# Feature tiles and seven products in a fixed order, and seven separate sums in the second layer, in a two-layer DiT trunk

## The chip, the cores and the metric

The kernel runs on one core of a Trainium2 chip. The metric is the device time of one execution in microseconds (us). Before the change three runs gave 1634.02, 1637.30 and 1638.63 us, a median of 1637.3 us.

## The reference

The reference is a trunk of two layers over 512 latent tokens and 256 context tokens of width 1024. Each layer has a mixer part (four head groups behind one input projection, one output projection) and an MLP with a squared ReLU, each with a modulated LayerNorm in front and a LayerNorm behind. The change lies in the MLP alone:

```
def channel_mlp(h, w1, w2):
    return jnp.square(jax.nn.relu(h @ w1)) @ w2      # 1024 -> 4096 -> 1024

x = layer_norm_affine(DN_ALPHA * x + m[2] * y, ln1_g[l], ln1_b[l])
f = channel_mlp(modulate(x, m[3], m[4]), w_ff1[l], w_ff2[l])
x = layer_norm_affine(DN_ALPHA * x + m[5] * f, ln2_g[l], ln2_b[l])
```

The second layer has no context tokens in its MLP, since only the latent stream is returned. So N, the number of tokens in the MLP, is 768 in the first layer and 512 in the second.

## The kernel before

All matrix products keep float32 accuracy by splitting each operand into a rounded part and a rest: `mm3` (L135) issues three matmuls (hi*hi, hi*lo, lo*hi) for each product of 128 rows. A weight tile therefore arrives by DMA as "raw", ScalarE copies it to "hi" (L162, L1307), and VectorE subtracts to get "lo" (L165, L1308).

The 4096 features of the MLP are worked in eight chunks of 512 (`ffn`, L1181). A **feature tile** (`ff1`, L1212) is 128 features for all tokens: 8 x 3 matmuls of 512 columns, and in the first layer 8 x 3 more of 256 columns for the context; ScalarE's ReLU reads it out of PSUM (L1199). Seven chunks, 0 to 6, of the second product go through a scheme with **seven products** in place of eight (Winograd's form of Strassen's): `operands` (L1256) squares the tiles on GpSimd (L1262), forms sums of halves of the tokens on GpSimd (L1281), and splits seven left operands (L1274 and L1275, tiles "fop"); `weights` (L1287) does the same with four quarters of the weight chunk (differences on GpSimd at L1312); `ff2_chunk` (L1323) multiplies. One product is HT blocks of 128 tokens (HT is 3 in the first layer, 2 in the second), each of 2 x 3 matmuls of 512 columns into one PSUM bank. Behind each bank VectorE adds it into SBUF (L1338), into one or two of the sums "acc" and "base"; the first time a sum is written ScalarE copies it (L1336). Per chunk that is 10 additions of 128x512 for each of the HT blocks, in both layers.

The last chunk is computed directly: four feature tiles, squared as hi and lo (`square`, L1201), and `ff2_tile` (L1371) with 12 matmuls for each tile of 128 tokens and 512 outputs, 12 such tiles in the first layer and 8 in the second. Before they can be added, the sums are finished: "base" is added (L1418), GpSimd multiplies by the gate row (L1419), and VectorE adds the residual "rawx", which comes back from DRAM (L1420). The residual loads, the last weights and the weights of the chunks share one pool of four raw buffers (`N_RAW`, tag "raw").

Who does what when: the kernel is written in program order and a scheduler orders the instructions of each engine ahead of time; each engine then runs its list in order. TensorE's order in this part is the scheduler's, too (`self.pin` is None). DMAs that go through `bcast_rows` (L1434) are issued from ScalarE's list and keep their place in program order; the gate rows of the second half of the layer come through it, by `rows2(0)`, right behind the first feature tiles. The lines that hold this:

```
    rs = ff1_first()
    big = [self.G([128, 1024], "base") for _ in range((HT + 1) // 2)]
    gl, gc = rows2(0)
    ...
    for c in range(NCH - 1):
        if c < NCH - 2:
            ops = operands(ff1(c + 1))
        ff2_chunk(c, left, acc, base, more)
    rs = ff1(NCH - 1)
```

Of the kernel before, what the change touches and what calls it, by code (L numbers as in the profile page):

```python
# [9 lines left out]
F32 = mybir.dt.float32  # L10
F32R = mybir.dt.float32r
AF = mybir.ActivationFunctionType
ALU = mybir.AluOpType
# [5 lines left out]
NL = 512  # L19
# [28 lines left out]
class Trunk:  # L48
# [105 lines left out]
    def load_w(self, pieces, shape, name, gate=None):  # L154

        nc = self.nc
        raw = self.pr.tile(shape, F32, name=self.nm("raw" + name), tag="raw")
# [1023 lines left out]
    def ffn(self, l, hL, hC, x, xc, rows2, mod2, done):  # L1181
# [6 lines left out]
        def ff1_w(f):  # L1188
            W = self.load_w([((slice(None),), w1[:, :, 128 * f:128 * f + 128])], [128, 8, 128], "w1",
                            self.gate if f < 8 else None)  # L1190
            return [[W[j][:, k, :] for j in range(2)] for k in range(KT)]
# [20 lines left out]
        def ff1(c):  # L1212
            rs = []
            for f in range(4 * c, 4 * c + 4):
                W = ff1_w(f)
                ps = self.P2("ff1")
                ff1_mm(ps[:, :NL], hL, 0, W)
                if full:
                    ff1_mm(ps[:, NL:NL + NC], hC, 0, W)
                r = self.T("relu", 768)  # L1220
                relu(r, 0, ps[:, :N])
                rs.append(r)
            return rs
# [32 lines left out]
        def operands(rs):  # L1256

            pool = nc.gpsimd  # L1260
            for r in rs:
                pool.tensor_tensor(out=r[:, :N], in0=r[:, :N], in1=r[:, :N], op=ALU.mult)  # L1262
            q = []
            for p in range(2):
                tmp = self.T("fsum", 768)
                e, o = rs[2 * p], rs[2 * p + 1]
                q.append((e[:, :half], o[:, :half], e[:, half:N], o[:, half:N], tmp[:, :half], tmp[:, half:N]))

            def halves(k):
                res = []  # L1270
                for v in q:
                    z = self.Z("fop")
                    hi, lo = z[:, :half], z[:, half:N]
                    nc.scalar.activation(out=hi, in_=v[k], func=AF.Copy)  # L1274
                    nc.vector.tensor_tensor(out=lo, in0=v[k], in1=hi.bitcast(F32), op=ALU.subtract)  # L1275
                    res.append((hi, lo))
                return res

            def sums(o, a, b, op):
                for v in q:  # L1280
                    pool.tensor_tensor(out=v[o], in0=v[a], in1=v[b], op=op)  # L1281

            yield halves(0)
            sums(4, 2, 3, ALU.add)
            yield halves(4)
            sums(5, 4, 0, ALU.subtract)
            yield halves(5)  # L1287
            sums(4, 1, 5, ALU.subtract)
            yield halves(4)
            sums(2, 0, 2, ALU.subtract)  # L1290
            yield halves(2)
            yield halves(1)
            yield halves(3)

        def weights(c):

            pool = nc.gpsimd
# [13 lines left out]
            def diff(o, a, b):  # L1311
                pool.tensor_tensor(out=o, in0=a, in1=b, op=ALU.subtract)  # L1312

            b11, b12, b22, b21 = raw(0, 0), raw(0, 1), raw(1, 1), raw(1, 0)
            yield halves(b11)
            diff(b11, b12, b11)
            yield halves(b11)
            diff(b11, b22, b11)
            yield halves(b11)
            diff(b12, b22, b12)  # L1320
            yield halves(b22)
            yield halves(b12)
            yield halves(b21)  # L1323
            diff(b21, b21, b11)
            yield halves(b21)

        def ff2_chunk(c, left, acc, base, more):


            B = weights(c)  # L1330
            seen = set()

            def add(ps, key, sl):
                if c == 0 and key not in seen:
                    seen.add(key)
                    nc.scalar.activation(out=sl, in_=ps, func=AF.Copy)  # L1336
                else:
                    nc.vector.tensor_tensor(out=sl, in0=ps, in1=sl, op=ALU.add)  # L1338

            for i, to in enumerate((("11", "B"), ("12", "22"), ("B",), ("12",), ("21", "22"), ("11",), ("21",))):  # L1340
                if i % 2 == 0:
                    banks = [self.PA("ff2") for _ in range(HT)]
                else:
                    big = self.P2("ff2")
                    banks = [big[:, 0:512], big[:, 512:1024]]
                    if HT > 2:
                        banks.append(self.PF("ff2") if i == 3 else self.P2("ff2")[:, 0:512])
                W, a = next(B), left[i]
                for t in range(HT):
                    for p in range(2):  # L1350
                        self.mm3(
                            banks[t], [h[:, 128 * t:128 * t + 128] for h in a[p]],
                            [h[:, p, :] for h in W], p == 0, p == 1,
                        )
                    for q in to:
                        if q == "B":
# [41 lines left out]
        for c in range(NCH - 1):  # L1398
            nxt, ops = [], None
            if c < NCH - 2:  # L1400
                ops = operands(ff1(c + 1))
                nxt += [next(ops), next(ops)]
# [262 lines left out]
```

## Time and profile before

| what | us |
|---|---|
| median of three runs | 1637.3 |
| the profiled execution | 1640.47 |
| its span, first to last instruction | 1638.4 |
| TensorE busy in the span | 1484.5 (91%) |
| VectorE busy | 1102.6 (67%) |
| ScalarE busy | 661.7 (40%) |
| GpSimd busy | 600.9 (37%) |
| chunk loop of the first layer, first tile of chunk 1 to first matmul of the last product | 436.8 to 921.3 |
| the same of the second layer | 1266.1 to 1595.5 |

The profile is one execution; it is 3.2 us longer than the median of the runs. Matmuls are pipelined in it: two in a row overlap, so the spacing of their starts, not their duration, tells what one costs. The chunk loops and the direct last chunk are more than half of the span.

### The profile page before, as it was taken

The numbers are of one execution on the slowest core, as the hardware profiler recorded it, in microseconds if no ns is written. First come the engines' busy times: TensorE is split into PE (matmuls) and PEld (weight loads), VectorE is DVE, ScalarE is ACT, GpSimd is POOL, SyncE is SP. The second block draws the span as 40 slices with busy tenths as digits, with TensorE's granted clock in tenths as the row PEclk, the third lists the DMA queues.
The fourth block names the chain that finished last, engine by engine and source line by source line (L and its number), as shares of the span: only waits on it lengthen the run. The fifth ranks groups of instructions, "written<-read, shape, count | busy, mean of one in ns | idle before, by whom it ended". The sixth has DMA issues, their size and how long they took to land. (4 is left out here: it accounts for less than half of the span.)

```text
span 1638.4 us, 23881 instructions
## 1 busy us (share of the span) xinstructions
PE 1484.5 (91%) x9228; PEld 1226.5 (75%) x9228; DVE 1102.6 (67%) x1811; ACT 661.7 (40%) x1207; POOL 600.9 (37%) x478
## 2 busy tenths in 40 slices
PE   5899889999999899999997989989989999898895
PEld 3689667787988687787876767867778778777674
DVE  3384655566574847648399589575465877678896
ACT  3433455425562323323221355355436643334331
POOL 1021333233363252432525151143242655443633
PEclk9999899999999999999999889999998999999997
DMA  8442366265212302123014423245265122233152
GB/s 287 142 117 63 122 217 193 80 223 179 78 39 65 98 29 80 39 64 91 28 62 128 130 78 116 65 149 162 86 217 179 52 89 91 81 100 103 52 154 77
DMA packets 150954, 180.45 MB, mean 110 GB/s; under 512 B 9096, under 2 KB 96568, under 8 KB 150840
## 3 DMA queue, kind: packets, MB, share of 16 engines
q1 hardware_dynamic: 140792, 160.42, 31.3%
q10 hardware_dynamic: 10048, 18.49, 3.4%
q8 instruction: 73, 1.20, 0.3%
q14 instruction: 41, 0.34, 0.1%
HBM read 169.43 MB, written 9.46 MB: 109 GB/s over the span
## 5 line engine op out<-in xcount | busy, mean ns | idle before, releaser
L133 PE MATMUL ff<-hiw,fop 128*128 128x512 f32 x980 | 325.0, 406 | 36.3 <-DVE acc L1338 35.6
L133 PEld LDWEIGHTS ff<-hiw,fop 128*128 128x128 f32 x980 | 191.3, 195 | 87.9 <-DVE acc L1338 25.3
L133 PE MATMUL ff<-hh,hiw 128*128 128x512 f32 (+1 forms) x672 | 241.6, 360 | 13.6 <-DVE acc L1338 9.5
L1308 DVE TENSOR_TENSOR low<-raww,hiw 128x1024 fp32r<-128x1024 f32 x98 | 136.7, 1397 | 159.7 <-ACT hiw L1307 159.4
L133 PE MATMUL ff<-hl,hiw 128*128 128x512 f32 (+1 forms) x672 | 240.4, 358 | 0.0
L133 PE MATMUL ff<-hh,low 128*128 128x512 f32 (+1 forms) x672 | 239.4, 356 | 0.7 <-DVE low L165 0.7
L1262 POOL TENSOR_TENSOR relu<-relu 128x768 f32<-128x768 f32 (+1 forms) x56 | 91.2, 1631 | 318.3 <-ACT relu L1199 318.3
L133 PE MATMUL ff<-low,fop 128*128 128x512 f32 x490 | 199.2, 406 | 6.7 <-DVE low L1308 6.7
L1307 ACT ACTIVATE hiw<-raww 128x1024 fp32r<-128x1024 f32 x98 | 103.2, 1060 | 231.6 <-PE ff L133 157.7
L1338 DVE TENSOR_TENSOR acc<-ff,acc 128x512 f32<-128x512 f32 x260 | 167.9, 676 | 12.3 <-PE ff L133 12.2
L1312 POOL TENSOR_TENSOR raww<-raww,raww 128x1024 f32<-128x1024 f32 x56 | 137.3, 2452 | 86.7 <-DVE low L1308 67.5
L133 PEld LDWEIGHTS ff<-hh,hiw 128*128 128x128 f32 x672 | 128.8, 192 | 36.0 <-issue 13.6
L133 PEld LDWEIGHTS ff<-hh,low 128*128 128x128 f32 x672 | 128.0, 190 | 19.2 <-DVE low L165 1.1
L133 PEld LDWEIGHTS ff<-hl,hiw 128*128 128x128 f32 x672 | 128.8, 192 | 18.0
L162 ACT ACTIVATE hiw<-raww 128x1024 fp32r<-128x1024 f32 x64 | 66.5, 1057 | 143.0 <-PE ff L133 103.2
L133 PEld LDWEIGHTS ff<-low,fop 128*128 128x128 f32 x490 | 95.5, 195 | 32.1 <-DVE low L1308 13.0
L547 POOL TENSOR_SCALAR p<-p,rec 128x768 f32<-128x768 f32 (+3 forms) x80 | 63.4, 796 | 143.1 <-DVE rec L546 133.4
L1275 DVE TENSOR_TENSOR fop<-relu,fop 128x384 fp32r<-128x384 f32 (+1 forms) x112 | 87.0, 801 | 39.9 <-ACT fop L1274 39.9
L165 DVE TENSOR_TENSOR low<-raww,hiw 128x1024 fp32r<-128x1024 f32 x64 | 82.0, 1289 | 14.6 <-ACT hiw L162 14.5
L133 PE MATMUL ada<-wada,sc 128*32 128x128 f32 x1536 | 62.4, 300 | 22.5 <-DMA wada<-in_w_ada 22.5
L1275 DVE TENSOR_TENSOR fop<-fsum,fop 128x384 fp32r<-128x384 f32 (+1 forms) x84 | 75.0, 914 | 7.3 <-ACT fop L1274 7.3
L1274 ACT ACTIVATE fop<-relu 128x384 fp32r<-128x384 f32 (+1 forms) x112 | 50.2, 466 | 68.1 <-POOL relu L1262 34.3
(362 smaller groups left out, 3237.7 us busy)
## 6 DMA issues: line engine op xcount, KB each, us to landing
raww<-in_w_ff SPq DMA_DIRECT2D x120, 512.0 KB, 4.2
wada<-in_w_ada SPq DMA_DIRECT2D x96, 512.0 KB, 4.6
rawwo<-in_w_out SPq DMA_DIRECT2D x16, 512.0 KB, 7.7
rawx<-xr SPq DMA_DIRECT2D x10, 512.0 KB, 3.4
rawz<-in_w_ff SPq DMA_DIRECT2D x8, 512.0 KB, 4.6
xr<-x SPq DMA_DIRECT2D x8, 512.0 KB, 5.1
rawwb<-in_w_in SPq DMA_DIRECT2D x12, 256.0 KB, 4.3
gate<-grow ACTq DMA_DIRECT2D x6, 512.0 KB, 7.2
```

What stands on the lines that cost most here:

```text
L133: return self.pinned(self.nc.tensor.matmul(out, lhsT, rhs, start=start, stop=stop))
L162: i = nc.scalar.activation(out=hi, in_=raw, func=AF.Copy)
L165: nc.vector.tensor_tensor(out=lo, in0=raw, in1=hi.bitcast(F32), op=ALU.subtract)
L547: nc.gpsimd.tensor_scalar(out=p[:, :keep], in0=p[:, :keep], scalar1=rec, scalar2=1.0, op0=ALU.mult, op1=ALU.mult)
L1262: pool.tensor_tensor(out=r[:, :N], in0=r[:, :N], in1=r[:, :N], op=ALU.mult)
L1274: nc.scalar.activation(out=hi, in_=v[k], func=AF.Copy)
L1275: nc.vector.tensor_tensor(out=lo, in0=v[k], in1=hi.bitcast(F32), op=ALU.subtract)
L1307: nc.scalar.activation(out=hi, in_=t, func=AF.Copy)
L1308: nc.vector.tensor_tensor(out=lo, in0=t, in1=hi.bitcast(F32), op=ALU.subtract)
L1312: pool.tensor_tensor(out=o, in0=a, in1=b, op=ALU.subtract)
L1338: nc.vector.tensor_tensor(out=sl, in0=ps, in1=sl, op=ALU.add)
```

## The change

- `ff1` becomes `ff1_tile`, one feature tile a call. The loop writes out an order for every chunk: "f01f23f45f6", where f is a feature tile of the next chunk and a digit is one of the seven products of this one. In chunk 6 the order is "01f23f456ff", and the feature tiles are those of the direct last chunk. `self.pin` is set over the loop, so TensorE runs in just this order.
- The raw weights of feature tiles in the loop come into pool "G" (4 buffers of 128x1024, shared with "base" and the gate rows) in place of the pool "raw". So that buffers of G are free, `rows2(0)`, the load of the gate rows, moves from the start of the loop to behind it.
- `operands` takes two tiles at a time, and the squares go from GpSimd to ScalarE.
- The seven products come in another order, with their sums in other places. In the second layer each product has a sum of its own, over all seven chunks (one addition a block in place of 10 for seven products); they are combined behind the loop by seven additions of 128x512 for each of two blocks. The first layer keeps its 10 additions a block.
- The last product's banks, and those of products 1, 3 and 5, come from other PSUM pools.

The core of the diff:

```diff
-        def ff1(c):
-            rs = []
-            for f in range(4 * c, 4 * c + 4):
-                W = ff1_w(f)
...
+        def ff1_tile(f, spare):
+
+            W = ff1_w(f, spare)
+            ps = self.P2("ff1")
...
-        raw = self.pr.tile(shape, F32, name=self.nm("raw" + name), tag="raw")
+        raw = self.G(shape, "raw" + name) if spare else self.pr.tile(
+            shape, F32, name=self.nm("raw" + name), tag="raw")
...
-            for r in rs:
-                pool.tensor_tensor(out=r[:, :N], in0=r[:, :N], in1=r[:, :N], op=ALU.mult)
+            for r in (e, o):
+                nc.scalar.activation(out=r[:, :N], in_=r[:, :N], func=AF.Square)
...
-            for i, to in enumerate((("11", "B"), ("12", "22"), ("B",), ("12",), ("21", "22"), ("11",), ("21",))):
+        TO = (("11", "B"), ("12",), ("11",), ("12", "22"), ("B",), ("21", "22"), ("21",)) if full else (
+            ("11",), ("12",), ("2",), ("22",), ("6",), ("7",), ("21",))
...
-        gl, gc = rows2(0)
...
+        self.pin = True
         for c in range(NCH - 1):
...
+            B = weights(c)
+            rs, nxt = [], []
+            order = "f01f23f45f6" if c < NCH - 2 else "01f23f456ff"
+            for o in order:
+                if o != "f":
+                    product(int(o), B, left, acc, base, seen)
+                    continue
+                rs.append(ff1_tile(4 * c + 4 + len(rs), True))
+                if c < NCH - 2 and len(rs) % 2 == 0:
+                    nxt.append(operands(*rs[-2:]))
             left = nxt
-
-        rs = ff1(NCH - 1)
+        self.pin = None
+
+        gl, gc = rows2(0)
+
+        def plus(o, a):
+            nc.vector.tensor_tensor(out=o, in0=o, in1=a, op=ALU.add)
+
+        for t in range(0 if full else HT):
+            c11, c12, c21, c22 = (place(acc, base, q, t) for q in ("11", "12", "21", "22"))
+            p2, p6, p7 = (base[q][t] for q in ("2", "6", "7"))
+            plus(p6, c11)
+            plus(c11, p2)
+            plus(c12, c22)
+            plus(c12, p6)
+            plus(p7, p6)
+            plus(c21, p7)
+            plus(c22, p7)
```

How this moves instructions is shown at three places. The first is TensorE's list in the first layer, inside chunk 1 (ff1 and ff2 are PSUM banks of a feature tile and of a product, hiw and low are weights, fop a left operand, hh and hl the layer's input). Before, behind two products, the last bank of one and the first of the next:

```order
L133 MATMUL ff2_1224_5788<-hiw2_1225_5790,fop_1139_5239 128x512
L133 MATMUL ff2_1237_5864<-low2_1239_5867,fop_1155_5322 128x512
L133 MATMUL ff2_1237_5864<-hiw2_1238_5866,fop_1155_5322 128x512
L133 MATMUL ff2_1237_5864<-hiw2_1238_5866,fop_1156_5325 128x512
L133 MATMUL ff2_1237_5864<-low2_1239_5867,fop_1156_5325 128x512
L133 MATMUL ff2_1229_5826<-hiw2_1232_5830,fop_1149_5283 128x512
L133 MATMUL ff2_1229_5826<-low2_1233_5831,fop_1149_5283 128x512
```

The same place in the changed kernel, behind products 0 and 1:

```order
L133 MATMUL ff2_1199_5585<-hiw2_1200_5587,fop_1137_5181 128x512
L133 MATMUL ff2_1199_5585<-hiw2_1200_5587,fop_1173_5442 128x512
L133 MATMUL ff2_1199_5585<-low2_1201_5588,fop_1173_5442 128x512
L133 MATMUL ff2_1199_5585<-hiw2_1200_5587,fop_1173_5442 128x512
L133 MATMUL ff1_1205_5618<-hh_884_4127,hiw1_1203_5614 128x512
L133 MATMUL ff1_1205_5618<-hl_885_4128,hiw1_1203_5614 128x512
L133 MATMUL ff1_1205_5618<-hh_884_4127,low1_1204_5615 128x512
```

Before, all seven products of a chunk follow one another, and four feature tiles follow these; now a feature tile stands between products 1 and 2, 3 and 4, 5 and 6, and 6 and the next 0.

The second place is ScalarE's list in the first layer where the gate rows are loaded (relu and fh are a feature tile and its squared hi part, gate and ln2g are rows broadcast from DRAM, hiw2 a split weight). Before, at the start of the loop:

```order
L1199 ACTIVATE relu_1046_4597<-ff1_1085_4868 128x256
L1199 ACTIVATE relu_1047_4599<-ff1_1085_4868 128x256
L1437 DMA gate_1088_4921<-grow_990_4403 128x1024
L1437 DMA gate_1089_4923<-grow_992_4405 128x1024
L1274 ACTIVATE fop_1101_4947<-relu_1046_4597 128x384
```

In the changed kernel, behind the loop:

```order
L1200 ACTIVATE relu_1594_8361<-ff1_1593_8312 128x768
L1204 ACTIVATE fh_1614_8471<-relu_1594_8361 128x768
L1200 ACTIVATE relu_1599_8418<-ff1_1598_8369 128x768
L1440 DMA gate_1600_8420<-grow_990_4403 128x1024
L1440 DMA gate_1601_8422<-grow_992_4405 128x1024
L1440 DMA ln2g_1608_8457<-in_ln2_g 128x1024
L1440 DMA ln2b_1609_8459<-in_ln2_b 128x1024
L1204 ACTIVATE fh_1616_8476<-relu_1599_8418 128x768
L163 ACTIVATE hiw2_1619_8483<-raww2_1618_8481 128x1024
```

The two gate loads stood behind the ReLUs of the first four tiles of the layer; now they stand behind the ReLU of its last, 32nd feature tile.

The third place is VectorE's list in the first layer at the end of the loop (fl is the lo part of a squared tile, rawx the residual, low2 the lo part of a weight of the direct last chunk). Before:

```order
L1420 TENSOR_TENSOR acc_1095_4935<-acc_1095_4935,rawx_1605_8439 128x1024
L1420 TENSOR_TENSOR acc_1096_4936<-acc_1096_4936,rawx_1606_8445 128x1024
L165 TENSOR_TENSOR low2_1620_8484<-raww2_1618_8481,hiw2_1619_8483 128x1024
L1420 TENSOR_TENSOR acc_1097_4937<-acc_1097_4937,rawx_1607_8451 128x1024
L1204 TENSOR_TENSOR relu_1586_8251<-relu_1586_8251 128x768
L1205 TENSOR_TENSOR fl_1611_8462<-relu_1586_8251,fh_1610_8461 128x768
```

In the changed kernel:

```order
L1205 TENSOR_TENSOR relu_1599_8418<-relu_1599_8418 128x768
L1206 TENSOR_TENSOR fl_1617_8477<-relu_1599_8418,fh_1616_8476 128x768
L1423 TENSOR_TENSOR acc_1088_4926<-acc_1088_4926,rawx_1602_8424 128x1024
L1423 TENSOR_TENSOR acc_1089_4927<-acc_1089_4927,rawx_1603_8429 128x1024
L1423 TENSOR_TENSOR acc_1090_4928<-acc_1090_4928,rawx_1604_8434 128x1024
L1423 TENSOR_TENSOR acc_1091_4929<-acc_1091_4929,rawx_1605_8439 128x1024
L1423 TENSOR_TENSOR acc_1092_4930<-acc_1092_4930,rawx_1606_8445 128x1024
L166 TENSOR_TENSOR low2_1620_8484<-raww2_1618_8481,hiw2_1619_8483 128x1024
L1423 TENSOR_TENSOR acc_1093_4931<-acc_1093_4931,rawx_1607_8451 128x1024
L166 TENSOR_TENSOR low2_1623_8490<-raww2_1621_8487,hiw2_1622_8489 128x1024
```

The six residual additions stood ahead of the squares of the layer's last four feature tiles; now they stand behind the square of the very last one, and the last weights' lo parts among and behind them.

## Rows read from the trace of the kernel before

**Rows 1.** The page's first part: busy us, share of span, instructions
```profile
PE 1484.5 (91%) x9228; PEld 1226.5 (75%) x9228; DVE 1102.6 (67%) x1811; ACT 661.7 (40%) x1207; POOL 600.9 (37%) x478
```
**Rows 2.** PE's waits in tile ff, 436.8 to 921.3: releaser, us, times
```profile
  DVE acc L1338: 23.9, 24
  ACT relu L1199: 4.0, 1
```
**Rows 3.** PE's waits in tile ff, 1266.1 to 1595.5: releaser, us, times
```profile
  DVE acc L1338: 21.2, 9
```
**Rows 4.** PE timeline: start, us, instruction, count, [idle before]; first matmuls of stretches
```profile
436.76 0.40 PE L133 MATMUL ff<-hh,hiw 128*128 128x512 f32 x1
...
453.44 0.40 PE L133 MATMUL ff<-hiw,fop 128*128 128x512 f32 x1
...
457.55 0.39 PE L133 MATMUL ff<-hh,hiw 128*128 128x512 f32 x1
...
602.88 0.40 PE L133 MATMUL ff<-hiw,fop 128*128 128x512 f32 x1
...
638.14 0.47 PE L133 MATMUL ff<-hh,hiw 128*128 128x512 f32 x1 [0.44 <-DVE acc L1338]
...
921.26 0.40 PE L133 MATMUL ff<-hiw,fh 128*128 128x512 f32 x1
...
1266.13 0.40 PE L133 MATMUL ff<-hh,hiw 128*128 128x512 f32 x1
...
1277.04 0.62 PE L133 MATMUL ff<-hiw,fop 128*128 128x512 f32 x2
...
1279.76 0.39 PE L133 MATMUL ff<-hh,hiw 128*128 128x512 f32 x1
...
1595.50 0.39 PE L133 MATMUL ff<-hiw,fh 128*128 128x512 f32 x1
```
**Rows 5.** Windows: stretch, length, busy us by engine, PEclk, DMA share, GB/s
```profile
630.00:633.00 3.00, 3.00 (x10) 2.38 (x9) 3.00 (x6) 0.00 (x0) 0.00 (x0) 0.62 0.69 177
```
**Rows 6.** By line: mean or ns min/median/max of one; additions, squares, gate products
```profile
L1338 DVE TENSOR_TENSOR acc<-ff,acc 128x512 f32<-128x512 f32 x260 | 167.9, 676 | 12.3 <-PE ff L133 12.2
L1262 POOL TENSOR_TENSOR relu<-relu 128x768 f32<-128x768 f32 (+1 forms) x56 | 91.2, 1631 | 318.3 <-ACT relu L1199 318.3
L1419 POOL TENSOR_TENSOR acc<-acc,gate x10: 2772/3304/3382, 870.5 to 1585.4; 128x1024 f32<-128x1024 f32 x10
L1420 DVE TENSOR_TENSOR acc<-acc,rawx x10: 1206/1217/3420, 879.0 to 1592.8; 128x1024 f32<-128x1024 f32 x10
```
**Rows 7.** PE timeline at the ends of the layers
```profile
902.07 0.80 PE L133 MATMUL ff<-hh,hiw 128*128 128x512 f32 x1 [4.00 <-ACT relu L1199]
...
958.54 0.39 PE L133 MATMUL ff<-hiw,fl 128*128 128x512 f32 x1
...
1623.02 0.39 PE L133 MATMUL ff<-hiw,fl 128*128 128x512 f32 x1
```
**Rows 8.** ACT timeline at the end of the first layer
```profile
900.26 1.06 ACT L162 ACTIVATE hiw<-raww 128x1024 fp32r<-128x1024 f32 x1 [25.72 <-DMA raww<-in_w_ff]
```
**Rows 9.** DMA: KB each, median us to landing (page); gate rows 436 to 470
```profile
raww<-in_w_ff SPq DMA_DIRECT2D x120, 512.0 KB, 4.2
gate<-grow ACTq DMA_DIRECT2D x6, 512.0 KB, 7.2
...
DMA to landing us min/median/max: 4.1/4.1/4.1
```
**Rows 10.** By line: splits of weights, squares on ACT, sums on POOL
```profile
L162 ACT ACTIVATE hiw<-raww 128x1024 fp32r<-128x1024 f32 x64 | 66.5, 1057 | 143.0 <-PE ff L133 103.2
L165 DVE TENSOR_TENSOR low<-raww,hiw 128x1024 fp32r<-128x1024 f32 x64 | 82.0, 1289 | 14.6 <-ACT hiw L162 14.5
L1203 ACT ACTIVATE fh<-relu x8: 632/732/848, 902.0 to 1598.9; 128x768 fp32r<-128x768 f32 x4, 128x512 fp32r<-128x512 f32 x4
L1281 POOL TENSOR_TENSOR fsum<-relu,relu x28: 732/1012/1713, 440.4 to 1528.0; 128x384 f32<-128x384 f32 x14, 128x256 f32<-128x256 f32 x14
```

More of the change, by code (lines that the diff above doesn't have):

```diff
@@ L1254, in ff1_first, with operands @@
             return rs
-        def operands(rs):
+        def operands(e, o):
             pool = nc.gpsimd
-            for r in rs:
-                pool.tensor_tensor(out=r[:, :N], in0=r[:, :N], in1=r[:, :N], op=ALU.mult)
[L1263 to L1293, printed above, removed]
@@ L1318, in weights @@
             diff(b11, b22, b11)
[L1319 to L1322, printed above, removed]
             yield halves(b21)
[L1324 to L1338, printed above, removed]
-            for i, to in enumerate((("11", "B"), ("12", "22"), ("B",), ("12",), ("21", "22"), ("11",), ("21",))):
[L1341 to L1356, printed above, removed]
-                            sl = base[t]
-                        else:
-                            n = int(q[1]) - 1
-                            sl = acc[HT * (int(q[0]) - 1) + t][:, 512 * n:512 * n + 512]
-                        add(banks[t], (q, t), sl)
-                more()
@@ new lines, in weights, with place, product @@
+            diff(b21, b21, b22)
+            for t in (b12, b22, b11, b21):
+                yield halves(t)
+        TO = (("11", "B"), ("12",), ("11",), ("12", "22"), ("B",), ("21", "22"), ("21",)) if full else (
+            ("11",), ("12",), ("2",), ("22",), ("6",), ("7",), ("21",))
+        def place(acc, base, q, t):
+            if len(q) == 1:
+                return base[q][t]
+            n = int(q[1]) - 1
+            return acc[HT * (int(q[0]) - 1) + t][:, 512 * n:512 * n + 512]
+        def product(i, B, left, acc, base, seen):
+            if i in (0, 2, 4, 6):
+                banks = [self.PA("ff2") for _ in range(HT)]
+            else:
+                big = self.P2("ff2")
+                banks = [big[:, 0:512], big[:, 512:1024]]
+                if HT > 2:
+                    banks.append(self.PF("ff2"))
+            W = next(B)
+            for t in range(HT):
+                ps = banks[t]
+                for p in range(2):
+                    self.mm3(
+                        ps, [h[:, 128 * t:128 * t + 128] for h in left[p][i]],
+                        [h[:, p, :] for h in W], p == 0, p == 1,
+                    )
+                for q in TO[i]:
+                    sl = place(acc, base, q, t)
+                    if (q, t) in seen:
+                        nc.vector.tensor_tensor(out=sl, in0=ps, in1=sl, op=ALU.add)
+                    else:
+                        seen.add((q, t))
+                        nc.scalar.activation(out=sl, in_=ps, func=AF.Copy)
@@ L1388, in ffn @@
         rs = ff1_first()
-        big = [self.G([128, 1024], "base") for _ in range((HT + 1) // 2)]
-        base = [big[t // 2][:, 512 * (t % 2):512 * (t % 2) + 512] for t in range(HT)]
-        gl, gc = rows2(0)
         xr = self.pd.tile([N, D], F32, name=self.nm("xr"), tag=self.nm("xr"))
@@ L1415, in ffn @@
             for n in range(2):
-                if j >= HT or n:
+                if full and (j >= HT or n):
                     sl = t[:, 512 * n:512 * n + 512]
-                    nc.vector.tensor_tensor(out=sl, in0=sl, in1=base[j % HT], op=ALU.add)
+                    nc.vector.tensor_tensor(out=sl, in0=sl, in1=base["B"][j % HT], op=ALU.add)
             nc.gpsimd.tensor_tensor(out=t, in0=t, in1=gl if j < LT else gc, op=ALU.mult)
```

64 lines of the change are left out of this document (39 added, 25 removed).

## The prediction, made before the run

> **What bounds the kernel now.** The page's first part comes first: TensorE is busy for 91% of the span, no other engine over 67% [rows 1]. So the time is TensorE's work, its waits and its clock, and the next view is what TensorE waits for in the chunk loops: VectorE's additions at L1338, 23.9 us in the first layer and 21.2 in the second, plus 4.0 once for a ReLU [rows 2, 3]. A bank can be written again only when its addition has read it, and seven products in a row fill banks faster than VectorE empties them.
>
> Waits are not the whole loss. Starts of matmuls give the price of undisturbed work [rows 4]: in the first layer two feature tiles take 453.44 - 436.76 = 16.68 us, so one costs 8.34, and the product behind them 457.55 - 453.44 = 4.11. In the second layer one feature tile costs (1277.04 - 1266.13) / 2 = 5.455 and a product 2.72. Later the seven products of one chunk take 638.14 - 602.88 = 35.26 us in place of 7 x 4.11 = 28.8. [...]
>
> A whole loop at undisturbed prices (28 feature tiles and 49 products) would be 28 x 8.34 + 49 x 4.11 = 434.9 us in the first layer; it takes 921.26 - 436.76 = 484.5, so 49.6 are lost. In the second it would be 28 x 5.455 + 49 x 2.72 = 286.0; it takes 329.4, and 43.4 are lost. **93.0 us** is therefore all that a better order of the loops can give.
>
> **The change: the order in the loops.** With a feature tile behind every two products, a bank's next use comes at least one feature tile later (8.34 or 5.46 us). One bank's additions are one or two of 0.676 us [rows 6]. In the first layer VectorE has 30 additions in a chunk as before, 20.3 us, but now over 62 us of TensorE work (4 x 8.34 + 7 x 4.11) rather than in a burst of 28.8. Two products of 3 blocks leave at most 12 additions, 8.1 us, beside the 8.34 that cover them. In the second layer a chunk has 14 additions in place of 20: 9.5 us, not 13.5. I count these waits as gone, and with them the low clock behind them.
>
> What stays is an estimate. At a loop's start the first product stands behind one feature tile and no longer behind two. It needs ReLU, a square of 0.73 and splits; the second needs four sums on GpSimd of 0.73 to 1.71 each [rows 10]. At the worst that is 0.73 + 4 x 1.71 = 7.6 us and two splits, against 8.3 and a product: some 4.5 us late in the first layer, 4 in the second. Between chunks 5 and 6 no feature tile stands in front of product 0, about 1 us in each layer; and 0.3 for each of the other 12 chunks or so. Together 14 us, from 4 (the start-up alone, half hidden) to 35 (2.5 for every chunk). The loops **gain 93 - 14 = 79**, bounds 58 and 89.
>
> **Squares.** 56 of 1.631 us leave GpSimd [rows 6]; on ScalarE one should cost 0.63 to 0.85, as L1203's squares do [rows 10]. ScalarE is 40% busy [rows 1], and 56 x 0.73 = 41 us lie beside TensorE's work: nothing. **Combination.** Behind the second loop VectorE does 14 additions where it did 6, 8 x 0.676 = 5.4 us more. They need the last products only, and two feature tiles (10.9 us) follow these: nothing, at the most 5. **Weights in G** need the same loads of 4.2 us [rows 9], with a tile's time for each to hide in: nothing.
>
> **The change: the gate rows, a new wait.** The two gate loads now stand in ScalarE's list behind the ReLU of the last feature tile. The residual's work stands behind them: a gate product on GpSimd, an addition of rawx on VectorE. The rawx loads hold all four raw buffers, and the last weights need the same buffers. So the first direct tile must wait for several gate products. Before, the loads had landed a whole loop earlier. What a late load does in this place the trace shows on a smaller scale: ScalarE's copy hiw waited 25.72 us for a raw load with ReLU behind it, and TensorE then idled 4.00 us [rows 7, 8].
>
> Call T the end of the last feature tile in the first layer. ReLU 0.8, issue 0.4 and landing 4.1 put the gate at T + 5.3; I take 5.5. (4.1 is what these loads took in an undisturbed stretch; the median of the kind is 7.2 [rows 9].) GpSimd's products follow at 2.77 to 3.38, say 3.15, the addition is 1.21 [rows 6]. The third buffer comes free at T + 5.5 + 3 x 3.15 + 1.2 = T + 16.2; a load of 4.2, hi 1.06 and lo 1.29 [rows 9, 10] put the first usable weight at T + 22.8. The two others follow 3.15 apart in their gate products; the fourth load needs the first one's buffer, so its lo is ready about T + 30.3. Two direct tiles wait for it, the second ends at T + 31.5, and ten more at 2.72 (12 matmuls, as many as a product of the second layer) give T + 58.7. Before, the twelve took 958.54 - 921.26 = 37.3 from first to last start [rows 4, 7]. That is 21 more, and a restart at the low clock adds about 1: **+22** (17 to 30).
>
> In the second layer there are four gate products: gate at T + 5.3, lo parts at 17.2, 20.3, 22.5 and 25.6, the second direct tile ends at 26.8, and six at 2.72 give T + 43. Before: 1623.02 - 1595.50 = 27.5 [rows 4, 7]. **+16** (12 to 22).
>
> **Sum.** -79 + 22 + 16 = -41. On the profiled execution that is 1640.5 - 41 = 1599.5; it was 3.2 longer than the median of the runs, so 1596.
>
> [...]
>
> **Rivals.** *The tails are hidden.* If the gate rows land and the raw buffers turn over while TensorE still has work, the loop's gain stays whole: 1640.5 - 79 - 3.2 = 1558. For it: only the list's order says that the loads are late. Against it: TensorE has nothing between the last feature tile and the direct tiles.
>
> *The loops keep their stalls in part.* VectorE also does all splits (a lo part of a weight is 1.29 us [rows 10]), which can stand ahead of an addition. If 24 to 40 us more stay lost, the gain is 55 to 39 and the tails take it: 1620 to 1636. Against it: 8.1 us of additions beside a cover of 8.34 is the tightest place, and most are looser.
>
> *Slower: operands come late in every chunk.* The squares and splits stand in ScalarE's list among the copies hiw of feature weights, which wait for loads into G; with "base" in two of its four buffers, two are left in the first layer. If a load is not ahead, a chunk pays 4.2 + 1.06 (+ 1.29) = 5.3 to 6.5 us [rows 9, 10], with product 0 or 1 of the next chunk idle behind it. It decides from 41 / 12 = 3.4 us for each of the 12 crossings; at 5 to 6.5 the time is 1656 to 1674. For it: the 25.72 us of [rows 8] are such a wait. Against it: two buffers against one tile in 15 us leave a load of 4.2 ample time.
>
> **How the numbers follow.** Forecast 0.72; tails hidden 0.11; stalls in part 0.10 (0.05 of it within 0.3%); slower 0.07. About 0.3%, 5 us, is what a measurement of this kernel can tell from no change. So faster 0.88, same 0.05, slower 0.07. The forecast's own bounds, 58 to 89 gained and 29 to 52 lost, give 1577 to 1631 with all ends at once; I take 1572 to 1622, which reaches a little towards the hidden tails and covers the near half of the stalls; left out are 1558, 1636 and the slower case.
>
> **What would show it.** Right: TensorE's waits for VectorE's additions in the two loops fall from 45 to under 10 us; the loops take some 442 and 294 us; behind each loop TensorE idles about 20 us, with the last weights as releaser, which came from raw buffers that GpSimd's gate products held; the direct tiles take some 59 and 43 us. Wrong: idle time in front of the first products of chunks (operands), or a ScalarE copy that waits for a load inside the loop; or no gap behind the loop.

## The result and the profile after

The changed kernel takes 1756.9 us (1752.8 to 1759.9) where the kernel before takes 1636.3 in the same sitting: **7.4% slower**, a ratio of 1.0735 with a 95% interval of 1.0707 to 1.0763. Forecast were 1596 us, 1572 to 1622, and a gain.

The page's first part of the changed kernel answers [rows 1]: TensorE works slightly longer than before (1511.0 us against 1484.5, for the same 9228 matmuls) in a span that is 120 us longer, and its share falls from 91 to 86%.

```profile
PE 1511.0 (86%) x9228; PEld 1245.6 (71%) x9228; DVE 1046.3 (60%) x1773; ACT 697.8 (40%) x1267; POOL 507.9 (29%) x422
```

What TensorE waits for in the two loops, answering [rows 2, 3] (releaser, us, times), first 437.1 to 966.5:

```profile
  DVE acc L1340: 50.4, 19
  ACT acc L1343: 5.0, 2
  DVE fop L1270: 1.2, 1
```

and 1339 to 1700:

```profile
  DVE acc L1340: 33.6, 18
  DVE fop L1270: 10.0, 7
  ACT fop L1269: 6.8, 7
  ACT acc L1343: 2.5, 3
```

The additions (L1340, L1338 before) were to be waited for no more; they cost 84.0 us of idle time now where they cost 45.1. The starts of matmuls answer [rows 4, 7]: the first and the last matmul of the first loop's feature tiles, the first and the last matmul of its direct tiles, and the same of the second layer.

```profile
437.15 0.40 PE L133 MATMUL ff<-hh,hiw 128*128 128x512 f32 x1
...
966.28 0.28 PE L133 MATMUL ff<-hh,low 128*128 128x256 f32 x1
988.18 0.80 PE L133 MATMUL ff<-hiw,fh 128*128 128x512 f32 x1 [21.62 <-ACT hiw L163]
...
1027.14 0.39 PE L133 MATMUL ff<-hiw,fl 128*128 128x512 f32 x1
...
1339.16 0.40 PE L133 MATMUL ff<-hh,hiw 128*128 128x512 f32 x1
...
1699.11 0.39 PE L133 MATMUL ff<-hh,low 128*128 128x512 f32 x1
1714.40 0.80 PE L133 MATMUL ff<-hiw,fh 128*128 128x512 f32 x1 [14.91 <-ACT hiw L163]
...
1741.60 0.39 PE L133 MATMUL ff<-hiw,fl 128*128 128x512 f32 x1
```

This divides the 119.6 us by which the span grew (a loop from its first to its last feature matmul, a tail from there to the last direct matmul):

| stretch | before | after | difference | forecast |
|---|---|---|---|---|
| first loop | 484.4 | 529.1 | +44.7 | about -43 |
| second loop | 329.1 | 360.0 | +30.9 | about -36 |
| first tail | 37.4 | 60.9 | +23.5 | +22 |
| second tail | 27.8 | 42.5 | +14.7 | +16 |
| all else | | | +5.8 | 0 |

The tails are as forecast. The loops carry the whole error: 79 us were to be gained and 75.6 are lost.

**Where a wait stands.** TensorE's first wait in chunk 1 of the first layer (start, us, then the idle time in brackets):

```profile
526.74 0.80 PE L133 MATMUL ff<-hiw,fop 128*128 128x512 f32 x1 [3.12 <-DVE acc L1340]
```

Product 0 begins at 517.99, and 24 matmuls of TensorE's list stand between there and this one: the 18 of product 0 and the first six of product 1. The wait is not between products. It stands in the middle of product 1, ahead of its second block. Products 1, 3 and 5 put their first two blocks into the two banks of one PSUM tile. In the kernel's list of TensorE's instructions, numbered in order and with the semaphores each waits for, the same place reads (2475 to 2480 are the first half of the tile ff2_1198, 2481 begins the second; DVE_49 counts VectorE's instructions):

```
2479 L133 MATMUL ff2_1198_5584<-low2_1201_5588,fop_1173_5442 128x512
2480 L133 MATMUL ff2_1198_5584<-hiw2_1200_5587,fop_1173_5442 128x512 [waits DVE_49]
2481 L133 MATMUL ff2_1198_5584<-hiw2_1200_5587,fop_1137_5181 128x512 [waits DVE_49]
2482 L133 MATMUL ff2_1198_5584<-low2_1201_5588,fop_1137_5181 128x512
```

Matmul 2481 uses weights and an operand that 2475 to 2480 have used already, so nothing that it reads can make it wait for VectorE (DVE). What lies between the halves in the program is the addition of the first half, and the count of DVE_49 that 2481 waits for is the one that this addition sets. So the program keeps the dependence for the tile as a whole: writing its second bank waits until the first has been read. Each of the 42 two-bank tiles of products has this link in the changed kernel, with no matmul between its halves, and all 37 waits for additions in the two loops stand at it. The five waits for ScalarE's copies (L1343, 7.5 us), which stand in place of additions where a sum is written first, stand at it too. What VectorE does meanwhile (start, us):

```profile
523.07 0.68 DVE L1340 TENSOR_TENSOR base<-ff,base 128x512 f32<-128x512 f32 x1
523.67 1.22 DVE L1291 TENSOR_TENSOR low<-raww,hiw 128x1024 fp32r<-128x1024 f32 x1
524.80 0.68 DVE L1340 TENSOR_TENSOR acc<-ff,acc 128x512 f32<-128x512 f32 x1
525.40 0.68 DVE L1340 TENSOR_TENSOR base<-ff,base 128x512 f32<-128x512 f32 x1
526.00 0.68 DVE L1340 TENSOR_TENSOR acc<-ff,acc 128x512 f32<-128x512 f32 x1
```

Product 0 has two additions for each block, 2 x 0.68 us, about what TensorE needs for a block (1.36); any split among them (low, 1.22) puts VectorE behind, and the addition of 526.00, on which product 1 depends, comes after all of it. The clock comes on top. The windows of the wait and of the four us behind it (length, busy us of PE, PEld, DVE, ACT and POOL, then PEclk, DMA share, GB/s):

```profile
523.50:526.70 3.20, 0.12 (x1) 0.00 (x0) 3.20 (x6) 0.87 (x2) 1.74 (x1) 0.84 0.00 0
526.70:530.70 4.00, 3.96 (x9) 3.14 (x10) 2.86 (x3) 0.00 (x0) 0.61 (x1) 0.50 0.28 75
```

VectorE is busy for all of the wait (3.20 of 3.20 us), and in the four us behind it TensorE works at a granted clock of 0.50. So a wait of 3.1 us makes a pair of products 13.2 us long in place of 8.2, as later chunks show, where the three pairs of a chunk take 13.2, 12.7 and 12.1: 13.3 us a chunk, of which 7.7 idle.

### The profile page after: what moved, and what is told of

Same layout as the page of the kernel before. It is cut to its first block, busy times and chain, and to the rows that moved or that the text cites. A ratio compares the mean times of both kernels' runs of the same rounds, so it can differ in the third digit from the quotient of the medians.

```text
span 1758.0 us, 23844 instructions
## 1 busy us (share of the span) xinstructions
PE 1511.0 (86%) x9228; PEld 1245.6 (71%) x9228; DVE 1046.3 (60%) x1773; ACT 697.8 (40%) x1267; POOL 507.9 (29%) x422
## 4 chain that ended last, share of the span: by engine, by line
PE 57%; DVE 18%; issue 8%; POOL 7%; ACT 5%; DMA 4%; SPq 0%; POOLq 0%; DVEq 0%; ACTq 0%
PE ff L133 29%; PE wo L133 6%; PE wb L133 3%; DVE acc L1340 3%; POOL raww L1295 3%; DVE fop L1270 2%; DVE low L1291 2%; PE o L133 2%; PE ada L133 2%; PE wa L133 2%; PE pT L189 2%; PE wp L133 2%; DMA wada<-in_w_ada 2%; PE wu L133 2%; ACT hiw L1290 2%
## 5 line engine op out<-in xcount | busy, mean ns | idle before, releaser
L133 PE MATMUL ff<-hiw,fop 128*128 128x512 f32 x980 | 356.4, 430 | 109.5 <-DVE acc L1340 84.0
L133 PEld LDWEIGHTS ff<-hiw,fop 128*128 128x128 f32 x980 | 203.4, 208 | 177.1 <-DVE acc L1340 99.3
L1291 DVE TENSOR_TENSOR low<-raww,hiw 128x1024 fp32r<-128x1024 f32 x98 | 137.4, 1404 | 217.6 <-ACT hiw L1290 217.6
L133 PE MATMUL ff<-low,fop 128*128 128x512 f32 x490 | 207.7, 424 | 0.0
L1340 DVE TENSOR_TENSOR acc<-ff,acc 128x512 f32<-128x512 f32 x228 | 152.3, 685 | 67.8 <-PE ff L133 65.0
L1270 DVE TENSOR_TENSOR fop<-relu,fop 128x384 fp32r<-128x384 f32 (+1 forms) x140 | 80.9, 605 | 65.3 <-ACT fop L1269 65.3
L133 PEld LDWEIGHTS ff<-low,fop 128*128 128x128 f32 x490 | 102.1, 208 | 19.5
L166 DVE TENSOR_TENSOR low<-raww,hiw 128x1024 fp32r<-128x1024 f32 x64 | 87.6, 1369 | 35.1 <-ACT hiw L163 35.1
L1269 ACT ACTIVATE fop<-relu 128x384 fp32r<-128x384 f32 (+1 forms) x140 | 58.3, 460 | 82.5 <-POOL relu L1277 82.1
L1274 POOL TENSOR_TENSOR fsum<-relu,relu 128x384 f32<-128x384 f32 (+1 forms) x28 | 25.4, 907 | 208.6 <-ACT relu L1261 208.6
L1200 ACT ACTIVATE relu<-ff 128x768 f32<-128x768 f32 (+2 forms) x76 | 45.4, 606 | 73.9 <-PE ff L133 73.8
```

The costliest lines, as they stand in the source:

```text
L133: return self.pinned(self.nc.tensor.matmul(out, lhsT, rhs, start=start, stop=stop))
L166: nc.vector.tensor_tensor(out=lo, in0=raw, in1=hi.bitcast(F32), op=ALU.subtract)
L1200: nc.scalar.activation(out=r[:, a:a + ps.shape[-1]], in_=ps, func=AF.Relu)
L1269: nc.scalar.activation(out=hi, in_=v, func=AF.Copy)
L1270: nc.vector.tensor_tensor(out=lo, in0=v, in1=hi.bitcast(F32), op=ALU.subtract)
L1291: nc.vector.tensor_tensor(out=lo, in0=t, in1=hi.bitcast(F32), op=ALU.subtract)
```

## The experiments

**Theory A**: the link between the two banks of a tile is what the fixed order exposes. Its rivals: **B**, VectorE is late with every bank; **C**, not the order but another part of the change (seven sums, squares, late gate rows) costs the loops. All runs are compared with the kernel before on the same chip; "loop" and "tail" are the stretches of the table above.

| run | us | ratio (95%) | loops | tails |
|---|---|---|---|---|
| changed kernel | 1756.9 | 1.0735 (1.0707 to 1.0763) | 529.1, 360.0 | 60.9, 42.5 |
| third_between | 1699.6 | 1.0364 (1.0335 to 1.0394) | 472.3, 360.3 | 61.4, 42.4 |
| adds_behind | 1626.6 | 0.9932 (0.9913 to 0.9952) | 438.9, 317.0 | 60.8, 42.6 |
| no_pin | 1596.9 | 0.9741 (0.9720 to 0.9762) | 436.2, 292.0 | 61.3, 42.7 |
| before_adds_behind | 1602.4 | 0.9772 (0.9745 to 0.9799) | 452.2, 318.4 | 37.4, 31.9 |
| early_fourth | 1602.2 | 0.9788 (0.9767 to 0.9808) | 442.9, 293.5 | 61.9, 42.5 |
| pool_squares | 1658.3 | 1.0139 (1.0106 to 1.0172) | 445.3, 344.9 | 62.4, 42.6 |
| one_sum | 1620.9 | 0.9907 (0.9874 to 0.9939) | 438.9, 313.6 | 60.8, 42.1 |
| adds_behind_gate | 1604.7 | 0.9822 (0.9780 to 0.9863) | 438.9, 317.1 | 48.5, 37.2 |
| no_pin_gate | 1570.4 | 0.9595 (0.9560 to 0.9630) | 441.6, 292.2 | 40.6, 31.7 |
| no_pin_gate_one_sum | 1581.8 | 0.9664 (0.9644 to 0.9685) | 443.7, 305.3 | 39.8, 29.0 |
| all_three | 1575.8 | 0.9627 (0.9605 to 0.9648) | 438.1, 286.5 | 46.9, 35.3 |

**1. The additions behind both halves.**

```diff
-                for q in TO[i]:
-                    sl = place(acc, base, q, t)
+                done_now = [t] if i % 2 == 0 or t == 2 else ([] if t == 0 else [0, 1])
+                for d in done_now:
+                    for q in TO[i]:
+                        sl = place(acc, base, q, d)
...
```

> The changed kernel, but the additions of the first half of a two-bank tile (products 1, 3 and 5) are written behind the matmuls of both halves. Theory A (the second half's matmuls wait for the addition of the first half, because both banks are one tile): the waits in the middle of products 1, 3 and 5 go (7.7 us idle a chunk in the first layer, some 5.5 in the second), with the half-clock matmuls behind them; first loop from 529 to 440-455 us, second from 360 to 310-325, time 1757 to 1620-1645. Rival B (VectorE is simply late with every bank, the tile does not matter): the wait moves to the next bank and the time stays within 1735-1757.

The waits for additions are gone from both loops; what is left in the first is 2.8 us, and in the second an operand (releaser, us, times; first loop, then second):

```profile
  DVE fop L1270: 1.2, 1
  ACT hiw L163: 1.1, 1
  DVE low L166: 0.5, 1
```

```profile
  DVE fop L1270: 10.4, 8
  ACT fop L1269: 9.5, 7
```

130 us are gained by moving some additions behind the next six matmuls. The order, the pin and all other parts are as in the changed kernel, and in this kernel's list no second half waits for its first any more, so B falls. The first loop, 438.9 us, is 4 over its undisturbed price of 434.9.

**2. The third block between the halves.**

```diff
-            for t in range(HT):
+            for t in ((0, 2, 1) if i % 2 and HT == 3 else range(HT)):
...
```

> The changed kernel, but products 1, 3 and 5 of the first layer write their third block (a bank of its own) between the two halves of the two-bank tile; the second layer has no third block and is unchanged. Theory A: each of the first layer's waits of 3.1, 2.6 and 2.0 us shrinks by the 1.36 us of the block in between, so 7 x 4.1 = 29 us of idle time less and part of the half clock, 30 to 45 us in all: 1712-1727, the second loop as before at 360. Rival B (VectorE late with every bank): no change, 1750-1760.

The first layer alone can do this, and the first loop alone changed (472.3 against 529.1; the second 360.3 against 360.0). The wait that was 3.12 us is now (start, us, idle):

```profile
519.70 0.50 PE L133 MATMUL ff<-hiw,fop 128*128 128x512 f32 x1 [1.75 <-DVE acc L1340]
...
537.73 0.50 PE L133 MATMUL ff<-hiw,fop 128*128 128x512 f32 x1 [1.24 <-DVE acc L1340]
...
555.19 0.50 PE L133 MATMUL ff<-hiw,fop 128*128 128x512 f32 x1 [0.67 <-DVE acc L1340]
```

The three waits of this chunk were 3.12, 2.58 and 2.03 in the changed kernel; they are shorter by 1.37, 1.34 and 1.36, the six matmuls (1.36 us) that stand between the halves now. The gain of 57 us is more than the 30 to 45 expected: the low clock behind the waits shrank more than I had allowed (outside its waits the first loop takes 443.9 us, and 472.5 in the changed kernel; the mean granted clock of the whole profiled execution is 0.956, and 0.936 in the changed kernel).

**3. No pin.**

```diff
-        self.pin = True
         for c in range(NCH - 1):
...
```

> The changed kernel without the pinned order of TensorE: the scheduler may again put other matmuls between the two halves of a tile. Theory A: most of the waits in the middle of products go, 1640-1690. Rival C (the seven sums, the squares on ScalarE or the late gate rows are what costs, not the order): within 20 us of 1757.

160 us are gained by leaving the order to the scheduler, and C falls for the loops: sums, squares and gate rows are those of the changed kernel. TensorE's list shows why, at product 1 of chunk 1 (ff2_1198 is its two-bank tile, ff2_1199 its third bank):

```
2480 L133 MATMUL ff2_1198_5584<-hiw2_1200_5587,fop_1173_5442 128x512 [waits DVE_49]
2481 L133 MATMUL ff2_1199_5585<-hiw2_1200_5587,fop_1137_5181 128x512
...
2514 L133 MATMUL ff2_1198_5584<-hiw2_1200_5587,fop_1137_5181 128x512 [waits DVE_49]
```

The link is there as before (2514 waits), but 33 matmuls stand between the halves, and the wait has passed before its turn. Over the 42 two-bank tiles the mean is 25. No wait for an addition is left in either loop, and at the link one of 1.9 us for ScalarE's copy in the first chunk.

**4. The same edit in the kernel before.**

```diff
-                    for q in to:
+                    done_now = [t] if i % 2 == 0 or t == 2 else ([] if t == 0 else [0, 1])
+                    for d in done_now:
+                        for q in to:
...
-                        add(banks[t], (q, t), sl)
+                            add(banks[d], (q, d), sl)
```

> The kernel before with the same edit (additions of a two-bank tile's first half behind the matmuls of both halves). Theory A: its 45 us of waits for VectorE's additions were the same link, so they fall under 15 us and the time from 1637 to 1570-1610. Rival B, and the reading of the prediction (seven products in a row fill banks faster than VectorE empties them): waits stay at 35-50 us, time 1625-1645.

In time A's expectation holds (1602), in waits it fails: 22.2 us of the 45.1 are left where under 15 were expected (first loop, then second):

```profile
  DVE acc L1338: 10.4, 7
```

```profile
  DVE acc L1338: 11.8, 10
```

Laid beside its list, the trace of the kernel before tells what each wait was for. Eight of the 33 waits of [rows 2, 3] stand at a tile's second half and are for the addition of its first: six in the first loop (5.4 us) and two in the second (2.4). The other 25, 37.3 us, stand at the first matmul of a tile and are for the addition of another tile. Examples of the link (555.76) and of the other kind (the two behind it):

```profile
555.76 0.50 PE L133 MATMUL ff<-hiw,fop 128*128 128x512 f32 x1 [0.98 <-DVE acc L1338]
...
559.82 0.49 PE L133 MATMUL ff<-hiw,fop 128*128 128x512 f32 x1 [1.16 <-DVE acc L1338]
...
1350.39 0.47 PE L133 MATMUL ff<-hiw,fop 128*128 128x512 f32 x1 [3.67 <-DVE acc L1338]
```

The first is ff2_1236's second half, which waits for its first; the second is ff2_1255, which waits for the addition of ff2_1244. So most of the waits of [rows 2, 3] were what the prediction read in them, banks that VectorE had not emptied. The link was in the kernel before too, but it cost 7.8 us in all, since the scheduler had put 23 other matmuls, on the mean of 42 tiles, between two halves. In this run all link waits are gone, and 15.1 us of the others with them. The edit also changed the order that the scheduler chose; what share of the gain each has isn't settled.

**5. The operand in the second loop.** What is left after experiment 1, 20 us of waits for fop, is nearly all product 1 of a chunk that waits for its left operand. That comes from the fourth feature tile by a square, four sums on GpSimd and a split, and in the second layer only product 6 (2.72 us), a feature tile (5.44) and product 0 stand between. The sums of one chunk and the split behind them, in the kernel of experiment 1 (GpSimd, then ScalarE; start, us):

```profile
1339.67 0.73 POOL L1274 TENSOR_TENSOR fsum<-relu,relu 128x256 f32<-128x256 f32 x1 [4.80 <-ACT relu L1261]
1340.37 2.39 POOL L1295 TENSOR_TENSOR raww<-raww,raww 128x1024 f32<-128x1024 f32 x1
1342.72 1.72 POOL L1275 TENSOR_TENSOR fsum<-fsum,relu 128x256 f32<-128x256 f32 x1
1344.40 0.73 POOL L1276 TENSOR_TENSOR relu<-relu 128x256 f32<-128x256 f32 x1
1345.09 2.40 POOL L1295 TENSOR_TENSOR raww<-raww,raww 128x1024 f32<-128x1024 f32 x1
1347.45 1.72 POOL L1277 TENSOR_TENSOR relu<-relu,fsum 128x256 f32<-128x256 f32 x1
...
1349.21 0.72 ACT L1269 ACTIVATE fop<-relu 128x256 fp32r<-128x256 f32 x2 [1.45 <-POOL relu L1277]
```

Two differences of weights, 4.8 us, stand in GpSimd's list among the sums, so that these take 9.5 us and not the 4.9 that they are busy. In this chunk product 1 then waits 0.54 us for ScalarE's half of the split and 1.42 for VectorE's (fop, L1270). VectorE's instruction takes 2.12 us there, from 1349.65 on, while GpSimd works on a third difference (1349.13 to 1351.48); the next such one takes 0.41.

```diff
-            order = "f01f23f45f6" if c < NCH - 2 else "01f23f456ff"
+            order = "f01f23ff456" if c < NCH - 2 else "01f23f456ff"
```

> The pinned kernel with the additions behind both halves, and the fourth feature tile of each chunk of the order placed behind product 3 instead of behind product 5 (f01f23ff456). Theory (the 20 us of idle time that are left in the second loop are product 1 waiting for the operand at the end of square, four GpSimd sums and split, behind the fourth tile; two products more, 5.4 us, between them cover it): the waits for ScalarE's and VectorE's fop fall from 20 to under 5 us, second loop from 327 to about 302 (as without the pin), 1627 to 1597-1607. Rival (the chain starts late for another reason, such as GpSimd's queue of weight differences): 1615-1628.

The second loop falls from 317.0 to 293.5 us, that of the kernel without the pin, and the waits for fop from 19.9 us to 2.8. Its waits (releaser, us, times):

```profile
  DVE acc L1342: 2.5, 1
  DVE fop L1270: 1.8, 2
  ACT fop L1269: 1.0, 1
```

**6. Squares on GpSimd again**, with the edit of experiment 1.

```diff
-                nc.scalar.activation(out=r[:, :N], in_=r[:, :N], func=AF.Square)
+                pool.tensor_tensor(out=r[:, :N], in0=r[:, :N], in1=r[:, :N], op=ALU.mult)
```

> The pinned kernel with the additions behind both halves, squares on GpSimd again. Theory (in the second loop product 1 waits some 2 us a chunk, with half clock behind it, for an operand at the end of a chain square, four sums, split; GpSimd squares lengthen that chain by 1 to 3 us a chunk, the first layer has room): 1632-1655. Rival (the squares are hidden on either engine): 1620-1631.

32 us slower than with squares on ScalarE (34 by the ratios), more than expected, and 28 of it in the second loop, where the waits for ScalarE's half of the operand's split alone are

```profile
  ACT fop L1269: 35.4, 7
```

5 us a chunk. In the fixed order the squares on ScalarE are no matter of cover: they shorten a chain that ends last.

**7. One sum less.** The second layer adds as the first does.

```diff
-        TO = (("11", "B"), ("12",), ("11",), ("12", "22"), ("B",), ("21", "22"), ("21",)) if full else (
-            ("11",), ("12",), ("2",), ("22",), ("6",), ("7",), ("21",))
+        TO = (("11", "B"), ("12",), ("11",), ("12", "22"), ("B",), ("21", "22"), ("21",))
...
```

> The pinned kernel with the additions behind both halves, and the second layer adds its products as the first one does (10 additions a block and chunk, no seven sums, no combination at the end). Theory (VectorE has room in the second loop, so the seven sums are worth next to nothing): 1620-1635. Rival (the seven sums carry the gain of the second layer, by 4.1 us of VectorE time a chunk): 1640-1660.

1620.9 against 1626.6: the intervals of the two ratios overlap, so under the pin the seven sums gain nothing that can be told. Without the pin and with the gate rows earlier it is otherwise:

> The kernel without the pin and with the gate rows earlier, and with the second layer's products added as in the first one (no seven sums, no combination). Theory (the seven sums are worth nothing where VectorE has room, and their combination stands in front of the gate products at the end): 1562-1572, no slower than 1570. Rival (without the pin VectorE's 4.1 us of additions a chunk come back as waits): 1580-1600.

1581.8 against 1570.4, and the intervals don't overlap: here the theory failed, and the seven sums are worth 11 us. The second loop is 305.3 us without them and 292.2 with them. In that layer the direct matmuls begin 8.3 us ahead of the last feature matmul here, so loop and tail overlap; together they are 10.4 us longer. TensorE idles 11.3 us in the loop and 3.4 with the seven sums. The waits are for VectorE's splits (4.3 us for L1291, 2.0 with the seven sums), once, at the link, for ScalarE's copy of a sum (3.3) and for ReLUs (2.6); no run takes them one by one.

**8. The gate rows ahead of the last two feature tiles.**

```diff
+                last = c == NCH - 2 and len(rs) >= 2
+                if last and len(rs) == 2:
+                    gl, gc = rows2(0)
-                rs.append(ff1_tile(4 * c + 4 + len(rs), True))
+                rs.append(ff1_tile(4 * c + 4 + len(rs), not last))
...
-        gl, gc = rows2(0)
```

> The changed kernel without the pin, and with the gate rows loaded ahead of the last two feature tiles of the loop rather than behind them; these two tiles take their raw weights from the pool of four raw buffers, so that pool G has room for the gate rows. Theory (the gaps of 21.7 and 14.9 us behind the loops are the gate rows' late load and the chain of gate products that holds the raw buffers): the gate products begin some 14 us before the last feature tile ends, the gaps shrink to 3-8 us each, and the time falls from 1597 to 1560-1577. Rival (the last weights are late for another reason, for instance the queue of loads): gaps as before, 1590-1602.

> The pinned kernel with the additions behind both halves, and the same earlier load of the gate rows. Theory: gaps of 21.6 and 14.8 us behind the loops shrink to 3-8, from 1627 to 1590-1607. Rival: 1620-1632.

Both came in as expected: 26.5 us without the pin and 22 with it (24 and 18 by the ratios, which go by the kernel before on each run's own chip). With the pin the tails keep 10.8 and 9.7 us of idle time, for the last weights and their splits. Without the pin the direct tiles follow the last feature matmul at once (in the first layer, start and us):

```profile
875.10 0.28 PE L133 MATMUL ff<-hh,low 128*128 128x256 f32 x1
875.22 0.40 PE L133 MATMUL ff<-hiw,fh 128*128 128x512 f32 x1
```

where the changed kernel waited 21.62 us. GpSimd's gate products of the first layer then begin 29 us ahead of that point:

```profile
846.29 5.85 POOL L1422 TENSOR_TENSOR acc<-acc,gate 128x1024 f32<-128x1024 f32 x2 [29.71 <-DVE acc L1421]
```

no_pin_gate beats both kernels: 1570.4 us, 4.0% under the kernel before.

**9. All three edits.**

> No pin, gate rows earlier, and the additions behind both halves. Theory (the link between the halves costs only where the order is fixed or VectorE late; without the pin there are no waits for additions left to remove): 1563-1576. Rival (the link still costs without the pin): 1545-1560.

1575.8, not to be told from no_pin_gate's 1570.4. The loops are 9 us shorter in sum, the tails 10 longer. In no_pin_gate a single wait stands at the link, 1.9 us for ScalarE's copy in the first chunk, so little was left to remove. The idle time in the loops falls from 9.0 us to 3.0, and that in the tails grows from 12.9 to 20.8, mostly waits for VectorE's splits of the last weights (L166).

## Why the prediction was wrong

**What bounds: right for most of the waits.** TensorE's waits for additions were read as banks that fill faster than VectorE empties them. That holds for 25 of the 33 waits, 37.3 of the 45.1 us (experiment 4). The other eight are the link. The prediction took the sum of the waits from the trace and the reason from the program, and never asked at which matmul of a product they stand.

**The order in the loops: the step that failed.** "With a feature tile behind every two products, a bank's next use comes at least one feature tile later ... I count these waits as gone." This came true for a bank's next use: no wait of that kind is left in the loops of the changed kernel. But the link is a wait of one product for itself, between two halves of a tile, and no feature tile can stand there. The pinned order takes away the 23 matmuls that stood there before, and VectorE, with additions and splits in front, comes late to the first half's addition. The waits at the link grow from 8 to 37, from about 1 us each to between 1.4 and 3.9, from 7.8 us to 84.0, and the clock falls behind them (0.50 in the four us behind the wait of 3.12). The prediction put this term at nothing.

The forecast gain was there to be had: without the pin the loops take 436.2 and 292.0 us, a gain of 85 where the prediction had 79, and with the tails' loss that kernel comes to 1596.9. That this meets the forecast of 1596 so closely is luck, since its order is the scheduler's and not the one that the prediction reasoned about.

**What stays in the loops: under-sized.** The start-up and the crossings were put at 14 us for both loops. With the link gone the first loop loses 4, but the second, at 317.0, loses 31, 20 of them idle for operands. The start-up itself, put at 4.5 and 4 us, cost 1.6 us of idle time in the first loop, for weights, and 2.8 in the second, for operands (experiment 1). Its 4.5 us do not follow from the terms beside them, 7.6 us and two splits against a feature tile and a product, 12.4. The crossings are what was too small: 0.3 us for most, where the second layer idles about 2 us or more in each, with some matmuls at the low clock behind (the mean granted clock of that loop is 0.97 in experiment 1, and 1.00 in its first loop). The rival "operands come late in every chunk" was right in this effect and wrong in its cause: ScalarE's split is released by GpSimd's last sum (experiment 5), not by a load. The prediction had the same chain, but counted it at a loop's start alone and left out the differences of weights among the sums.

**Squares and combination.** Squares at nothing: with the fixed order and the additions behind both halves they are worth 32 us (experiment 6). The seven sums at nothing: so under the pin, 11 us without it (experiment 7).

**The gate rows: right, in mechanism and size.** +22 and +16 were forecast, +23.5 and +14.7 measured; the first usable weight was put at T + 22.8, and the first direct matmul starts 988.18 - 966.28 = 21.9 after the start of the last feature matmul. Loading the rows earlier gives 20.7 and 11.0 of it back (experiment 8, without the pin). The gate products begin when the gate row lands:

```profile
970.71 18.17 POOL L1422 TENSOR_TENSOR acc<-acc,gate 128x1024 f32<-128x1024 f32 x6 [78.82 <-DMA gate<-grow]
```

That is T + 4.2, where T + 5.5 was forecast, while the additions behind them took longer than forecast (see the residual). That these two errors nearly cancel is luck.

The "low clock" that adds about 1 us to this sum is in the kernel before [rows 5], 0.62 over three us; no run shows the 1 us by itself. In the changed kernel the granted clock is 0.50 behind both waits, from 988.2 to 996.2 and from 1714.4 to 1718.4. From 991.74 to 996.44 matmuls of 128x512 start 0.43 us apart, and 0.23 apart from 999.26 on, some 2.2 us more for these eleven; in the second tail it is 1.0 for five.

**The residual.** The additions of rawx, 1.21 us each before [rows 6], have a mean of 2.93 in the changed kernel, where they stand between gate products:

```profile
L1423 DVE TENSOR_TENSOR acc<-acc,rawx 128x1024 f32<-128x1024 f32 x10 | 28.8, 2927 | 5.5 <-POOL acc L1422 5.5
```

The eight that run beside gate products take 16.47 us (five, from 973.49 on) and 9.92 (three, from 1706.26 on), 3.3 each; the other two start behind the last gate product, at 991.02 and 1717.23, and take 1.21 each. What makes the eight longer isn't shown. The six gate products of the first layer took 18.17 us, 3.03 each, where the prediction's sum has 3.15.

**The two banks.** That the list holds a wait of a tile's second bank for its first, and that the order of writing (experiment 1) takes the 84.0 us of waits away, agrees with a link made by how the program keeps its tiles. Whether TensorE can write the one bank while VectorE reads the other isn't shown: no run here had the two engines at the two banks of one such tile at once.

**Open.** 5.8 us of the 119.6 lie outside the four stretches, 4.4 of them between the first layer's last direct matmul and the second loop; what makes them isn't settled.

## What to carry to other kernels

Before an order is fixed, look at what the scheduler had put between two instructions that depend on each other, and where in its group the waiting matmul stands: work "behind" a product does not cover a wait inside it. A program can keep the dependences of a tile of two banks as one, as here, so write both halves before either is read out; giving each bank its own tile would be another way, which no run here tried. A cause read from the program for a sum of waits is to be checked at single waits: two kinds stood under one name here, and the change removed the larger and multiplied the smaller. A fixed order needs each chain (ReLU, square, sums, split) set against the cover of every layer, the smallest one above all.

## What was not expected of the hardware

A short wait cost more than its idle time: 3.1 us of idle time made a pair of products 5.0 us longer, since the clock of the following four us was granted at 0.50 (526.70 to 530.70); by that clock 2.0 of the 5.0 us are lost there, an estimate. Waits cut to 1.75 and 1.24 us (experiment 2) saved 57 us in the first loop, of which the idle time is 28 (56.6 against 28.4 us idle). The other 29 lie outside the waits (472.5 us against 443.9), and the mean granted clock of the execution rose from 0.936 to 0.956: the clock gave back as much as the waits.
